# A 32-byte gap ahead of the pool that holds the two parts of the weights

## Chip, core and metric

The kernel runs on one core of one Trainium2 chip. The metric is device time in microseconds (us) of one execution, the median of several runs. TensorE (PE in the profile, PEld for its weight loads) multiplies, ScalarE (ACT) and VectorE (DVE) compute on what lies in SBUF and PSUM, and SyncE (SP) issues most transfers.

## What is computed

The reference is a trunk of two layers on one sequence of 256 tokens, model width 1024. All arrays are float32.

```
for l in range(2):
    x = x + 0.5 * swiglu(rmsnorm(x), w_gate, w_up, w_down)      # 1024 -> 2816 -> 1024
    h = rmsnorm(x)
    proj = h @ w_in          # [q | k | v | lru x | lru gate | memory q | 3 branch gates]
    A = window_attention(q, k, v)          # 8 heads of 64, 2 kv heads
    R = rg_lru(conv(lru x)) * gelu(lru gate)    # linear recurrence over tokens
    C = memory_attention(memory q, rmsnorm(mem) @ w_mem_kv)     # 4 heads of 128
    x = x + (g0 * (A @ w_attn_out) + g1 * (R @ w_lru_out) + g2 * (C @ w_mem_out)) @ w_out
    x = x + 0.5 * swiglu(rmsnorm(x), w_gate2, w_up2, w_down2)
return rmsnorm(x)
```

## The kernel before

Activations are kept feature-major: features on the 128 partitions, the 256 tokens along the row. Every large product is cut into weight blocks of 128 x 128. There are 3,456 of them, packed in the order of use in DRAM; eight stand side by side in a slab of 128 x 1024, so there are 432 slabs.

A product keeps float32 accuracy with two parts for each factor. A value is rounded to the type float32r (the "hi" part), and what is missing is a second float32r number (the "lo" part). A slab arrives in a stage tile `st` (line 179, from SP's queue, up to five slabs ahead). In `prep`, ScalarE writes `whi` (line 194) and VectorE then writes `wlo` (line 195), three slabs ahead of their use:

```
nc.scalar.activation(hi[:, c], st[:, c], AF.Copy)
nc.vector.tensor_tensor(lo[:, c], st[:, c], hi[:, c].bitcast(F32), op=ALU.subtract)
```

Activations are held by the class `Halves`: for each 128 features 256 columns of hi and beside them 256 of lo. `gemm` then spends two matmuls on a block (lines 219 and 220): hi weights against both parts of the activations (512 columns), and lo weights against the hi part (256 columns):

```
mm(both, hi, X.both(k), start=(k == 0), stop=False)
mm(out[:, 0, :], lo, X.hi(k), start=False, stop=(k == n - 1))
```

In both the weights are the stationary operand, which is loaded into the array (LDWEIGHTS in the profile, one ahead of each matmul), and the activations are the moving one, which streams through it a column at a time. Two more places use three matmuls of 256 columns on a block, again with the weights stationary: `singles` at the end (lines 236 to 238) and the gates of the recurrent branch (lines 675 to 677). In the memory's values (lines 622 to 624) it is the other way round: there the activations `xs` are stationary and 512 columns of weights move. The attention's own products (line 946 is one) are in plain float32, with neither operand in `whi` or `wlo`.

The order of the work is written out by hand: `block` prepares the slabs and advances a clock of tasks by one at each slab, and evictions, norms and attention hang on that clock.

Tiles lie in SBUF pool behind pool, in the order of the lines in `pools`, and every tile's row takes a multiple of 32 bytes. The first pool begins at byte 16,512 of a partition, which is a multiple of 64, and its first tile `pk` takes 1,056 bytes (16.5 times 64). From there on all large tiles begin 32 bytes past a multiple of 64: `whi` at 187,168 and four more at steps of 4,096, `wlo` at 207,648 and four more. The activations' tiles (21,792 and steps of 8,192) and the stage tiles (166,688 and steps of 4,096) do too. Blocks in a slab are 512 bytes apart, and parts of an activation tile 1,024 or 2,048, so no slice changes that remainder.

Of the kernel before, what the change touches and what calls it, by code (L numbers as in the profile page):

```python
# [19 lines left out]
F32 = mybir.dt.float32  # L20
# [74 lines left out]
class Trunk:  # L95
# [17 lines left out]
    def pools(self, ctx):  # L113
        tc = self.tc
        e = ctx.enter_context
        self.pc = e(tc.tile_pool(name="const", bufs=1))
        self.pbig = e(tc.tile_pool(name="big", bufs=14))
        self.ph4 = e(tc.tile_pool(name="h4", bufs=3))
        self.ps2 = e(tc.tile_pool(name="s2", bufs=4))
        self.ps1 = e(tc.tile_pool(name="s1", bufs=3))  # L120
        self.psm = e(tc.tile_pool(name="sm", bufs=2))
        self.pst = e(tc.tile_pool(name="stage", bufs=5))
        self.phl = e(tc.tile_pool(name="hl", bufs=5))
        self.pmm = e(tc.tile_pool(name="mm", bufs=3, space=bass.MemoryType.PSUM))
        self.patt = e(tc.tile_pool(name="att", bufs=2, space=bass.MemoryType.PSUM))
# [931 lines left out]
```

## Time and profile before

| | |
|---|---|
| runs | 1290.47, 1281.79, 1282.45 us; median 1282.45 |
| profiled execution, its own time | 1282.87 us |
| its span, first to last instruction | 1281.1 us |
| mean granted clock of TensorE | 0.997 of full |
| TensorE matmuls busy | 1265.4 us, 99% |
| weight loads (beside matmuls) | 1104.4 us, 86% |
| VectorE, ScalarE busy | 985.7 us (77%), 761.3 us (59%) |

The profiled execution lies 0.42 us (0.03%) above the median, and 1.8 us of it lie around its span. A matmul's record is longer than its share of the engine: records overlap, since the next matmul starts while the one before it drains. What a matmul costs is therefore read from the distance of two starts (its pitch), not from its record.

### The profile page before, as it was taken

Reading aid. Unit: us, or ns where it says so; the run is one execution under the profiler, and the core shown is the slowest. Engines: PE = TensorE matmul, PEld = TensorE weight load, DVE = VectorE, ACT = ScalarE, POOL = GpSimd, SP = SyncE. Lnnn points to the kernel's source line nnn. Section 1 sums busy time; section 2 is a strip of 40 time slices with the busy share of each in tenths; the row PEclk is TensorE's granted clock in tenths of the full one; section 3 lists DMA queues with packets and bytes.
Section 4 is the critical chain, followed back from the end, with each engine's and each line's share of the span. In section 5 each row is a group of like instructions: output and inputs, shape, how many; then the busy total and the mean of one; then the engine's idle time right before and its main releaser. Section 6 shows DMA issues by size and latency. Waiting matters only on the chain.

```text
span 1281.1 us, 19099 instructions
## 1 busy us (share of the span) xinstructions
PE 1265.4 (99%) x7318; PEld 1104.4 (86%) x7318; DVE 985.7 (77%) x1406; ACT 761.3 (59%) x1134; POOL 0.3 (0%) x5
## 2 busy tenths in 40 slices
PE   8999999999999999999999999999999999999997
PEld 7888888888888888888888888888888888888886
DVE  7788766888789987677678775669887898876754
ACT  5656544588577565555456564447867675655542
POOL 0000000000000000000000000000000000000000
PEclk9999999999999999999999999999999999999998
DMA  8665665555445566666656665564554465665651
GB/s 288 209 189 167 214 183 179 172 175 166 144 131 187 187 197 189 195 187 202 194 184 208 189 188 195 167 204 156 183 165 132 148 199 180 197 195 185 195 184 48
DMA packets 64748, 232.40 MB, mean 181 GB/s; under 512 B 7313, under 2 KB 7441, under 8 KB 64401
## 3 DMA queue, kind: packets, MB, share of 16 engines
q1 hardware_dynamic: 64224, 230.65, 57.2%
q8 instruction: 58, 0.95, 0.3%
q10 hardware_dynamic: 432, 0.53, 0.1%
q14 instruction: 34, 0.27, 0.1%
HBM read 230.10 MB, written 1.05 MB: 180 GB/s over the span
## 4 chain that ended last, share of the span: by engine, by line
PE 90%; DVE 5%; ACT 3%; issue 1%; DMA 1%; SPq 0%; DVEq 0%; ACTq 0%
PE pd L219 12%; PE pg L219 11%; PE pu L219 11%; PE pd L220 6%; PE pgt L219 6%; PE pu L220 6%; PE pg L220 6%; PE pbr L219 5%; PE pgt L220 3%; DVE wlo L195 2%; PE pyr L219 2%; PE pwo L219 2%; PE pbr L220 2%; PE pxr L219 2%; PE pgu L219 2%; PE pcq L219 1%
## 5 line engine op out<-in xcount | busy, mean ns | idle before, releaser
L195 DVE TENSOR_TENSOR wlo<-st,whi 128x1024 fp32r<-128x1024 f32 (+2 forms) x438 | 524.6, 1206 | 238.1 <-ACT whi L194 238.0
L194 ACT ACTIVATE whi<-st 128x1024 fp32r<-128x1024 f32 (+2 forms) x438 | 443.5, 1045 | 39.5 <-PE pd L219 20.5
L219 PE MATMUL pd<-h,whi 128*128 128x512 f32 x660 | 230.1, 393 | 0.0
L219 PE MATMUL pg<-xs,whi 128*128 128x512 f32 x640 | 225.2, 394 | 0.0
L219 PE MATMUL pu<-xs,whi 128*128 128x512 f32 x640 | 225.1, 393 | 0.0
L220 PE MATMUL pd<-h,wlo 128*128 128x256 f32 x660 | 184.9, 280 | 0.0
L220 PE MATMUL pg<-xs,wlo 128*128 128x256 f32 x640 | 179.3, 280 | 0.8 <-DVE wlo L195 0.8
L220 PE MATMUL pu<-xs,wlo 128*128 128x256 f32 x640 | 179.3, 280 | 0.0
L219 PEld LDWEIGHTS pd<-h,whi 128*128 128x128 f32 x660 | 123.6, 187 | 28.1
L219 PEld LDWEIGHTS pg<-xs,whi 128*128 128x128 f32 x640 | 119.9, 187 | 27.0
L219 PEld LDWEIGHTS pu<-xs,whi 128*128 128x128 f32 x640 | 119.8, 187 | 26.9
L219 PE MATMUL pgt<-xs,whi 128*128 128x512 f32 x384 | 139.2, 405 | 0.0
L220 PEld LDWEIGHTS pd<-h,wlo 128*128 128x128 f32 x660 | 124.7, 189 | 0.0
L220 PEld LDWEIGHTS pg<-xs,wlo 128*128 128x128 f32 x640 | 120.9, 189 | 1.1 <-DVE wlo L195 1.1
L220 PEld LDWEIGHTS pu<-xs,wlo 128*128 128x128 f32 x640 | 121.0, 189 | 0.0
L220 PE MATMUL pgt<-xs,wlo 128*128 128x256 f32 x384 | 107.6, 280 | 0.0
L219 PEld LDWEIGHTS pgt<-xs,whi 128*128 128x128 f32 x384 | 72.1, 188 | 19.5 <-issue 3.0
L258 ACT COPY g<-pg 128x512 f32<-128x512 f32 x40 | 23.5, 586 | 99.7 <-PE pg L220 92.9
L220 PEld LDWEIGHTS pgt<-xs,wlo 128*128 128x128 f32 x384 | 72.5, 189 | 0.2
L270 ACT ACTIVATE h<-u 128x512 fp32r<-128x512 f32 x44 | 27.8, 632 | 46.2 <-DVE u L523 43.9
L320 ACT ACTIVATE xs<-x,pk 128x256 fp32r<-128x256 f32 x40 | 18.7, 503 | 49.2 <-DVE x L559 21.6
L219 PE MATMUL pgu<-xs,whi 128*128 128x512 f32 x128 | 44.7, 394 | 1.2 <-DVE xs L324 1.2
(237 smaller groups left out, 2053.5 us busy)
## 6 DMA issues: line engine op xcount, KB each, us to landing
st<-wpack SPq DMA_DIRECT2D x428, 512.0 KB, 3.8
st<-wpack SPq DMA_DIRECT2D x8, 256.0 KB, 4.9
mem<-memT SPq DMA_DIRECT2D x2, 1024.0 KB, 6.7
x<-xT SPq DMA_DIRECT2D x4, 256.0 KB, 5.0
outT<-xg SPq DMA_DIRECT2D x2, 256.0 KB, 2.6
outT<-xg ACTq DMA_DIRECT2D x2, 256.0 KB, 2.7
cst<-cst SPq DMA_DIRECT2D x1, 320.0 KB, 7.8
pk<-pk SPq DMA_DIRECT2D x1, 128.0 KB, 7.5
```

Source lines behind the costliest of these rows:

```text
L194: nc.scalar.activation(hi[:, c], st[:, c], AF.Copy)
L195: nc.vector.tensor_tensor(lo[:, c], st[:, c], hi[:, c].bitcast(F32), op=ALU.subtract)
L219: mm(both, hi, X.both(k), start=(k == 0), stop=False)
L220: mm(out[:, 0, :], lo, X.hi(k), start=False, stop=(k == n - 1))
L258: self.nc.scalar.copy(dst, ps[:, :, 1, :])
L270: hi = lambda: self.nc.scalar.activation(X.hi(k, n), src, AF.Copy)
L320: self.t.nc.scalar.activation(self.xs.hi(k), x[:, k, :], AF.Copy, scale=self.t.vec(self.v, self.l, k))
```

## The change

One line is added to `pools`. It opens a pool of its own, with one tile of 8 float32 (32 bytes) in a partition that nothing reads or writes, between the stage tiles and the pool `hl` of the weights' parts.

```diff
         self.pst = e(tc.tile_pool(name="stage", bufs=5))
+        e(tc.tile_pool(name="gap", bufs=1)).tile([128, 8], F32, name="gap")
         self.phl = e(tc.tile_pool(name="hl", bufs=5))
```

In the built program `whi` then begins at 187,200 and `wlo` at 207,680 and at steps of 4,096 from there: multiples of 64. All tiles ahead of the pool keep their places, and nothing in SBUF lies behind it. The instructions, their order on every engine and what they wait for are the same as before; only the addresses in those that read or write `whi` and `wlo` differ.

## Rows read from the trace of the kernel before

**Rows 1.** The page: engines (busy, share of the span, instructions), and the chain by engine.
```profile
PE 1265.4 (99%) x7318; PEld 1104.4 (86%) x7318; DVE 985.7 (77%) x1406; ACT 761.3 (59%) x1134; POOL 0.3 (0%) x5
PE 90%; DVE 5%; ACT 3%; issue 1%; DMA 1%; SPq 0%; DVEq 0%; ACTq 0%
```

**Rows 2.** Busy time by windows, matmuls of line 219 alone, then line 220 alone, whole span.
```profile
0.00:1281.10 1281.10, 1164.72 (x3316) 621.52 (x3316) 1.00 0.58 181
0.00:1281.10 1281.10, 927.86 (x3316) 625.88 (x3316) 1.00 0.58 181
```

**Rows 3.** Timeline of TensorE at 576 us: start, length of the record, instruction.
```profile
575.71 0.39 PE L219 MATMUL pu<-xs,whi 128*128 128x512 f32 x1
575.94 0.28 PE L220 MATMUL pu<-xs,wlo 128*128 128x256 f32 x1
576.05 0.39 PE L219 MATMUL pu<-xs,whi 128*128 128x512 f32 x1
...
577.79 0.39 PE L219 MATMUL pu<-xs,whi 128*128 128x512 f32 x1
```

**Rows 4.** The same at 150 us.
```profile
149.76 0.40 PE L219 MATMUL pd<-h,whi 128*128 128x512 f32 x1
150.00 0.28 PE L220 MATMUL pd<-h,wlo 128*128 128x256 f32 x1
150.12 0.40 PE L219 MATMUL pd<-h,whi 128*128 128x512 f32 x1
...
150.82 0.40 PE L219 MATMUL pd<-h,whi 128*128 128x512 f32 x1
```

**Rows 5.** Windows, line 219: busy matmuls (count), loads (count), granted clock, DMA share, GB/s.
```profile
100.00:190.00 90.00, 90.00 (x255) 47.82 (x256) 1.00 0.60 188
500.00:640.00 140.00, 140.00 (x405) 75.55 (x404) 1.00 0.63 193
```

**Rows 6.** Timeline of TensorE, float32r matmuls of 512 columns alone (838 us).
```profile
837.84 0.39 PE L622 MATMUL mv<-whi,xs 128*128 128x512 f32 x1
838.07 0.39 PE L623 MATMUL mv<-wlo,xs 128*128 128x512 f32 x1
...
838.52 0.39 PE L622 MATMUL mv<-whi,xs 128*128 128x512 f32 x1
```

**Rows 7.** Timeline of TensorE, float32r matmuls of 256 columns alone (1262 us).
```profile
1262.12 0.28 PE L236 MATMUL pd<-h,whi 128*128 128x256 f32 x1
1262.24 0.28 PE L237 MATMUL pd<-h,whi 128*128 128x256 f32 x1
...
1262.48 0.28 PE L236 MATMUL pd<-h,whi 128*128 128x256 f32 x1
```

**Rows 8.** Plain float32: sixteen records in a timeline row, and the group of line 946.
```profile
367.55 3.62 PE L946 MATMUL mv<-MT,mkv 128*128 128x256 f32 x16
L946 PE MATMUL mv<-MT,mkv x32: 379/379/379, 367.6 to 998.7; 128*128 128x256 f32 x32
```

**Rows 9.** Groups of lines 236 and 675: count, duration ns least/median/most, first and last start.
```profile
L236 PE MATMUL pd<-h,whi x44: 279/283/283, 1254.2 to 1269.7; 128*128 128x256 f32 x44
L675 PE MATMUL lg<-xcs,whi x32: 279/283/285, 254.5 to 905.9; 128*128 128x256 f32 x32
```

**Rows 10.** The page's costliest groups: the two steps that write the weights' parts.
```profile
L195 DVE TENSOR_TENSOR wlo<-st,whi 128x1024 fp32r<-128x1024 f32 (+2 forms) x438 | 524.6, 1206 | 238.1 <-ACT whi L194 238.0
L194 ACT ACTIVATE whi<-st 128x1024 fp32r<-128x1024 f32 (+2 forms) x438 | 443.5, 1045 | 39.5 <-PE pd L219 20.5
```

**Rows 11.** TensorE's waits: who, for whom, us in total, times, longest.
```profile
PE rst L305 <- DVE r L298: 2.1, 2, 1.3
PE pg L220 <- DVE wlo L195: 0.8, 1, 0.8
PE pgu L220 <- DVE wlo L195: 0.2, 1, 0.2
```

## The prediction

> **What bounds the kernel now.** The page comes first: TensorE is busy for 1265.4 of 1281.1 us and the chain of waits lies on it for 90% [rows 1]. So at most 15.7 us of the span are idle time of TensorE. The list of its waits agrees: the longest entry is 2.1 us, and for the weights' parts it waits 1.0 us in all [rows 11]. No transfer and no other engine sets the end. What counts is how fast TensorE goes from one matmul to the next while it never waits, and that is read from the distance of the starts.
>
> Line 219 and line 220 have 3,316 matmuls each [rows 2], so 3,316 of the 3,456 blocks go through `gemm`. At 576 us six blocks take 577.79 - 575.71 = 2.08 us, 346.7 ns a block [rows 3]. At 150 us three blocks take 1.06 us, 353.3 ns a block [rows 4]. These are two steady paces, not noise. Between 500 and 640 us there are 404 starts of line 219 (405 records, one of them begun earlier), 140.00 / 404 = 346.5 ns. Between 100 and 190 us there are 254, 354.3 ns, at a granted clock of 1.00, its 2.4 GHz level, in both [rows 5]. The starts of line 219 through the whole trace, read in the same way, give 1,068 blocks at the longer pace, some 2,100 at the shorter, and about a hundred in between or at a stop. The rows above are samples of the two.
>
> What would a block cost if columns alone counted? Matmuls of 512 columns alone follow each other at 0.68 / 3 = 226.7 ns [rows 6], those of 256 columns at 0.36 / 3 = 120.0 ns [rows 7]. The difference is 106.7 ns for 256 columns, 0.417 ns a column, one at each beat of 2.4 GHz. That leaves 226.7 - 512 x 0.417 = 13.3 ns, and likewise 120.0 - 106.7 = 13.3 ns: **a surcharge of 13.3 ns for each matmul with its load**, whatever its length. A block of `gemm` has 768 columns, 320.0 ns, and two surcharges, 26.7: the 346.7 of the shorter pace. The longer pace has 6.7 ns more a block, which is the time of 16 columns, and 16 columns of float32 are 64 bytes of a row. The plain float32 matmuls, which have a load each too, show almost no surcharge: (3.62 - 0.379) / 15 = 216.1 ns [rows 8] for 256 columns at twice the column time, 213.3, so 2.7 ns. Their operands lie 32 bytes past a multiple of 64 as well. So neither a load as such nor that address costs 13 ns; the surcharge belongs to operands read at float32r's full rate.
>
> **The change part by part.** (1) The stationary operand of 3,316 x 2 matmuls in `gemm` [rows 2], 3 x 44 in the last product and 3 x 32 in the recurrent gates [rows 9] begins on a multiple of 64: 6,860 matmuls. In all but the 96 of lines 622 to 624 the moving operand keeps its place. Columns and loads stay as many. The open price is what the start of the stationary row does to the 13.3 ns, and the trace has no float32r load from a multiple of 64. Bounds from the nearest rows: at best the surcharge vanishes, 6,860 x 13.3 = 91.5 us; at worst it grows by the one quantum that the trace shows, 6.7 ns, for each load, 6,860 x 6.7 = 45.7 us more. I take zero. The reason is the evenness of the surcharge: it is exactly 32 columns' time where 128 weights are loaded for 256 columns and where they are loaded for 512, a whole fraction of the 128 weights. A load that paid for the 32 bytes by which its 512 bytes are out of step would rather show a remainder, 9 pieces of 64 bytes where 8 would do.
>
> The trace thus shows 13.3 ns for a load of 128 weights. The Trainium skill, on the page "TensorE: Matmul & The Clock Gate" in the section "Weight-path perf modes — Fast Weight Load (FWL) and DoubleRow", tells of a mode that fetches 128 weights as four parallel chunks of 32 columns, for types other than FP32. An estimate by that page is 32 columns, 13.3 ns, whatever the address, so zero from this change; the trace agrees in the number, though no row tells the type that the load is treated as. The page "SBUF — State Buffer", section "Door 1: The DMA port swizzle", has SBUF in lines of 16 bytes. By it 32 past a multiple of 64 is the start of a line already, and the same 32 lines are read before and after: zero again. What no row shows is whether TensorE reads in such lines.
>
> (2) Which of the two paces a stretch falls into may change. It is set after a stop and then kept: 254 blocks in 90 us without a return to the other [rows 5]. If every block went at the shorter pace, 1,068 x 6.7 = 7.1 us would be saved; I take zero and keep it for the range.
>
> (3) ScalarE writes `whi` and VectorE reads `whi` and writes `wlo` at the new addresses: 443.5 and 524.6 us in all [rows 10]. VectorE is idle for 1281.1 - 985.7 = 295 us and ScalarE for 520 [rows 1]. If both steps took a tenth more, 44 and 52 us, that would lie in this idle time; if a tenth less, TensorE's waits for them would lose a part of their 1.0 us [rows 11]. Nothing on the path, below half a microsecond on either side. The slabs have a margin: eight blocks at 346.7 ns take 2.8 us, a `wlo` 1.2.
>
> (4) The gap's tile is never used: zero instructions, no wait, no transfer.
>
> The sum against the profiled execution is 1282.9 + 0 = 1282.9 us; its distance to the median, 0.4 us, is kept, which gives 1282 us.
>
> **The rivals.** *A piece of 64 bytes less.* TensorE may fetch rows in pieces of 64 bytes. Out of step, a load needs nine pieces and the moving row one more as well, and the 13.3 ns would be two such extra pieces of 16 columns each. With the stationary row in step, one goes: 6.7 ns x 6,860 = 45.7 us, 1237 us. For it speaks that both paces are multiples of 16 columns' time above 768 (64 and 80) and that at half the rate, in plain float32, the surcharge is hidden. Against it speaks that the load's ninth piece need not stand in the way of the moving row at all. If only one of a block's two loads gains, it is half of that, 1260 us. If the whole surcharge hangs on the load's start, 91.5 us go, 1191 us; at that pace a slab takes 8 x 320 = 2.6 us, still above the 1.2 us of VectorE's step, so TensorE would remain the bound.
>
> *The longer pace everywhere.* Before, both streams begin 32 bytes past a multiple of 64, so their fetches keep one phase to each other. After it they are half a piece apart. If that makes load and stream collide once more a block, as in the stretches at 353.3 ns, then the 3,316 - 1,068 = 2,248 blocks that escape it now pay 6.7 ns: 15.0 us, 1297 us. It decides once more than about 85 in 100 of these blocks change (12.8 us are 1%). For it speaks that the longer pace exists and holds for long stretches; against it, that nothing in the rows ties it to an address: each stretch of rows 5 runs through over thirty slabs, through all five buffers of `whi`, at one pace. With one more collision at every load it would be 45.7 us, 1328 us.
>
> *The change doesn't do what it says.* Excluded: the addresses in the built program are multiples of 64.
>
> **How the numbers follow.** The surcharge stays, 1275 to 1290 us with some shift between the two paces: 46%. A piece less at each load, 1237 us: 21%; at one of two, 1260 us: 10%; all of it, 1191 us: 5%. The longer pace everywhere, 1297 us: 10%; a piece more at each load, 1328 us: 8%. The range from 1234 to 1299 us leaves out the two outer cases, 13%. A measurement of this kernel can tell about 1% (13 us) from no change: faster by more than that 36%, within it 46%, slower 18%.
>
> **What would show it.** In the changed kernel the starts of lines 219 and 220 decide alone. The forecast holds if matmuls of 256 columns in line 236 still follow at 120.0 ns and blocks at 346.7 or 353.3. The first rival shows as 113.3 ns in line 236 and 333.3 ns a block; the second as 353.3 everywhere at unchanged 120.0. Lines 622 to 624, where the weights move and `xs` is stationary, tell which stream pays: their 226.7 ns should stay if the stationary row's start matters alone. Lines 194 and 195 should keep 1,045 and 1,206 ns. What makes the forecast wrong is the reading of 32 columns as a price of the weights' count; it rests on one number that two mechanisms can give.

## The result, and the profile after

The changed kernel takes 1292.36 us (median of 6 runs, 1291.81 to 1295.65) against 1282.6 (6 runs, 1281.79 to 1290.47): 0.81% slower, ratio 1.0081, 95% interval 1.0064 to 1.0098. The forecast was 1282. The profiled execution took 1292.42 us, 9.55 more than that of before.

The page after, engines and the chain by engine, answers to [rows 1]:

```profile
PE 1275.7 (99%) x7318; PEld 1107.7 (86%) x7318; DVE 985.7 (76%) x1406; ACT 762.5 (59%) x1134; POOL 0.3 (0%) x5
...
PE 92%; DVE 4%; ACT 2%; issue 1%; DMA 1%; SPq 0%; DVEq 0%; ACTq 0%
```

TensorE has 10.3 us more of busy time, ScalarE 1.2 us more and VectorE the same as before. All line numbers behind the added line are one higher: `gemm` is now on lines 220 and 221. The groups of `prep` and TensorE's waits, after, answer to [rows 10, 11]:

```profile
L196 DVE TENSOR_TENSOR wlo<-st,whi 128x1024 fp32r<-128x1024 f32 (+2 forms) x438 | 524.7, 1206 | 247.6 <-ACT whi L195 247.0
L195 ACT ACTIVATE whi<-st 128x1024 fp32r<-128x1024 f32 (+2 forms) x438 | 444.6, 1047 | 40.4 <-PE pd L220 20.0
```
```profile
PE rst L306 <- DVE r L299: 2.0, 2, 1.3
...
PE pgu L221 <- DVE wlo L196: 0.2, 1, 0.2
```

Nothing there. The time is in the pitch of the blocks. The same two windows as [rows 5], matmuls of line 220:

```profile
100.00:190.00 90.00, 90.00 (x260) 48.68 (x261) 1.00 0.60 192
500.00:640.00 140.00, 140.00 (x397) 74.34 (x396) 1.00 0.60 190
```

The stretch at 100 us held 255 records and now holds 260, the one at 500 us held 405 and now holds 397. The two have changed places: one sped up, the other slowed down. The timeline of TensorE after shows the steps, at 576 us (against [rows 3]) and at 150 us (against [rows 4]):

```profile
575.85 0.40 PE L220 MATMUL pu<-xs,whi 128*128 128x512 f32 x1
...
576.21 0.39 PE L220 MATMUL pu<-xs,whi 128*128 128x512 f32 x1
...
576.55 0.40 PE L220 MATMUL pu<-xs,whi 128*128 128x512 f32 x1
...
577.26 0.40 PE L220 MATMUL pu<-xs,whi 128*128 128x512 f32 x1
```
```profile
149.88 0.39 PE L220 MATMUL pd<-h,whi 128*128 128x512 f32 x1
...
150.91 0.39 PE L220 MATMUL pd<-h,whi 128*128 128x512 f32 x1
```

Four blocks take 1.41 us at 576 us, in steps of about 0.36 and 0.35 in turn: 353 ns a block, where it had been 346.7. Three blocks take 1.03 us at 150 us, where they had taken 1.06; starts are shown to 10 ns, so the pace is better read from the window, 90.00 / 260 = 346 ns. Read through the whole trace by the prediction's count, the starts give (some twenty blocks next to restarts can be counted one way or the other):

| blocks | before | after |
|---|---|---|
| at 346.7 ns | 2,099 | 591 |
| at 353.3 ns | 1,068 | 2,557 |
| in between | 44 | 63 |
| at a stop | 52 (24.8 us) | 52 (24.0 us) |

Net, 1,489 more blocks at the longer pace are 1,489 x 6.67 = 9.9 us, the stops give back 0.8; the span grew by 9.5. By stretches (start in us: blocks at ns a block), those of 95 blocks and more:

```
before  30:103@353  76:375@353  221:96@353  397:207@347  476:511@347  660:511@347  849:96@353  1025:207@347  1103:435@347
after   29:103@353  76:375@347  218:96@347  394:207@353  474:511@353  661:511@353  854:96@353  1030:207@353  1110:435@353
```

Two stretches got better and five got worse. Within these stretches the pace never changes; they are separated by the plain float32 matmuls of norms and attention, or by a wait.

The matmuls of one length alone moved too. After, 512 columns (against [rows 6]) and 256 columns (against [rows 7]):

```profile
845.64 0.40 PE L623 MATMUL mv<-whi,xs 128*128 128x512 f32 x1
...
847.50 0.39 PE L625 MATMUL mv<-whi,xs 128*128 128x512 f32 x1
```
```profile
1270.05 0.28 PE L237 MATMUL pd<-h,whi 128*128 128x256 f32 x1
...
1270.76 0.28 PE L237 MATMUL pd<-h,whi 128*128 128x256 f32 x1
```

Eight matmuls of 512 columns in 1.86 us are 232.5 ns each (226.7 before), six of 256 in 0.71 us are 118.3 (120.0 before). With 213.3 and 106.7 ns for the columns, the surcharge that was 13.3 ns in both is now 19.2 in the one and 11.7 in the other. On the 96 and 132 matmuls concerned this makes 0.6 us more and 0.2 us less.

### The profile page after: what moved, and what is told of

Same layout as the page of the kernel before. It is cut to its first block, busy times and chain, and to the rows that moved or that the text cites. A ratio compares the mean times of both kernels' runs of the same rounds, so it can differ in the third digit from the quotient of the medians.

```text
span 1290.6 us, 19099 instructions
## 1 busy us (share of the span) xinstructions
PE 1275.7 (99%) x7318; PEld 1107.7 (86%) x7318; DVE 985.7 (76%) x1406; ACT 762.5 (59%) x1134; POOL 0.3 (0%) x5
## 4 chain that ended last, share of the span: by engine, by line
PE 92%; DVE 4%; ACT 2%; issue 1%; DMA 1%; SPq 0%; DVEq 0%; ACTq 0%
PE pd L220 12%; PE pg L220 11%; PE pu L220 11%; PE pgt L220 7%; PE pd L221 6%; PE pu L221 6%; PE pg L221 6%; PE pbr L220 5%; PE pgt L221 3%; PE pbr L221 2%; PE pyr L220 2%; PE pwo L220 2%; DVE wlo L196 2%; PE pgu L220 2%; PE pxr L220 2%; PE pwo L221 1%
## 5 line engine op out<-in xcount | busy, mean ns | idle before, releaser
L196 DVE TENSOR_TENSOR wlo<-st,whi 128x1024 fp32r<-128x1024 f32 (+2 forms) x438 | 524.7, 1206 | 247.6 <-ACT whi L195 247.0
L195 ACT ACTIVATE whi<-st 128x1024 fp32r<-128x1024 f32 (+2 forms) x438 | 444.6, 1047 | 40.4 <-PE pd L220 20.0
L220 PE MATMUL pu<-xs,whi 128*128 128x512 f32 x640 | 227.8, 397 | 0.0
```

## The experiments

**Theories.** Theory P said that two paces exist at any address, that a restart settles which one a stretch takes, and that a new address only deals the restarts anew. A restart here is the first block behind plain float32 matmuls or a wait. Its rival S said that the half piece of 64 bytes between stationary and moving rows brings on the longer pace. Later theories took up what was left of both. In every count below a block's pace is read as above.

**First round: other addresses, and one other restart.** Edits, each against the kernel before or after:

```diff
 e1_gap64 (after)
-        e(tc.tile_pool(name="gap", bufs=1)).tile([128, 8], F32, name="gap")
+        e(tc.tile_pool(name="gap", bufs=1)).tile([128, 16], F32, name="gap")
 e2_all64 (before)
+        e(tc.tile_pool(name="gap", bufs=1)).tile([128, 8], F32, name="gap")
         self.pbig = e(tc.tile_pool(name="big", bufs=14))
 e3_moving64 (after)
+        e(tc.tile_pool(name="gap0", bufs=1)).tile([128, 8], F32, name="gap0")
         self.pbig = e(tc.tile_pool(name="big", bufs=14))
 e4_before_extra (before), in rstd_b behind the loop
+        self.nc.tensor.matmul(ps[:, 256:264], r[:, 0:1].to_broadcast([128, 128]), self.ident[:, 0:8],
+                              start=True, stop=True)
```

> The gap is 64 bytes instead of 32, so the stationary rows lie 64 bytes further on than before the change and again 32 past a multiple of 64, like the moving rows. Theory P (pace): a stretch of blocks goes at 346.7 or 353.3 ns a block at any start address, which of the two is settled when it restarts after plain float32 matmuls, and a new address only deals these restarts anew; the time may then be anything between 1275 us (all at 346.7) and 1298 us (all at 353.3), and the long stretches at 353.3 are others than before. Theory S (step): it is the half piece between stationary and moving rows that brings on the longer pace; then this kernel is the one before, 1282 to 1283 us, with the stretches of 374 blocks at 76 us and 95 blocks at 221 us at 353.3 and those of 510, 510 and 434 at 346.7.

> The 32-byte gap stands ahead of the pool of the activations' large tiles, so moving and stationary rows both begin on multiples of 64. Theory P: 346.7 and 353.3 ns a block as ever, mixed anew, 1275 to 1298 us. Theory S: both rows in step with each other as before the change, 1282 to 1283 us with the stretches of before. The prediction's rival of pieces of 64 bytes: the moving row's extra piece goes, so a block takes 320 to 333 ns and the kernel 1190 to 1237 us.

> One 32-byte gap ahead of the activations' large tiles and a second one ahead of the weights' parts, so the moving rows begin on multiples of 64 and the stationary rows 32 past one. Theory P: 1275 to 1298 us, paces mixed anew. Theory S: half a piece apart as in the changed kernel, so about 1292 us, with 353.3 ns in the stretches of 510, 510 and 434 blocks. Rival of pieces: the moving row alone pays, 1237 us.

> The addresses of before; one more plain float32 matmul of 8 columns stands behind the two that broadcast each norm, its result read by nobody, so that the array restarts a few tens of ns later after each norm. It costs 9 places by less than 0.25 us, at most 2 us, if nothing else moves. Theory P: the stretches that begin behind a norm (374, 95, 510, 510, 434 blocks) are dealt anew, each change of pace worth 6.7 ns a block, 2.5 us for 374 and 3.4 us for 510 blocks; some of them now go at another pace than before. Theory S: addresses are unchanged, so all keep the pace of before and the time is 1282 to 1285 us.

| run | us | ratio to before (interval) | blocks at 346.7 / 353.3 |
|---|---|---|---|
| e1_gap64 | 1295.63 | 1.0102 (1.0072 to 1.0133) | 1 / 3,197 |
| e2_all64 | 1290.56 | 1.0061 (1.0031 to 1.0090) | 664 / 2,498 |
| e3_moving64 | 1294.45 | 1.0087 (1.0055 to 1.0119) | 245 / 2,885 |
| e4_before_extra | 1290.69 | 1.0048 (1.0021 to 1.0076) | 1,032 / 2,140 |

S falls twice: with 64 bytes the remainder is that of before, yet not one long stretch keeps the shorter pace; and e4, with no address changed, is 0.48% slower, and its 1,072 more blocks at the longer pace (7.1 us) account for the 7.2 us by which its span grew. The rival of pieces falls too: in e2, with all these rows on multiples of 64, no stretch goes below 346.7 ns a block. The windows of line 220, of e1_gap64 and then (line 219) of e4_before_extra:

```profile
500.00:640.00 140.00, 140.00 (x397) 74.48 (x397) 1.00 0.61 189
```
```profile
500.00:640.00 140.00, 140.00 (x398) 74.48 (x397) 1.00 0.61 188
1120.00:1200.00 80.00, 80.00 (x232) 43.20 (x231) 1.00 0.61 191
```

Eight small matmuls have turned the stretches of 511 blocks to the longer pace (397 records where [rows 5] had 405), and left the last one at the shorter (232 records in 80 us are 346 ns).

**Second round: counting restarts.** Nine long stretches are too few to tell odds from chance. A probe puts a plain float32 matmul of 4 to 97 columns ahead of every product of `pair`, 354 in all; its result is overwritten by the product.

```diff
+        self.restarts = 0
...
         for m in range(2):
+            n = 4 + 3 * (self.restarts % 32)
+            self.restarts += 1
+            self.nc.tensor.matmul(ps[:, m, 0, 0:n], self.ident, self.ident[:, 0:n], start=True, stop=True)
             self.gemm(ps[:, m, :, :], mk(m), X)
```

It runs on the addresses of before (p0), on those of the change (p32), of e1 (p64) and of e2 (q0); the last three, with all pools moved by 32 bytes (q1) and gaps of 96 and 128 bytes (p96, p128), came after the third round. Each probe was run once.

> A probe: ahead of each product of `pair` stands one more plain float32 matmul, of 4 to 97 columns in turn, into the part of the PSUM tile that the product overwrites. It adds some 350 restarts with different delays, so that the share of restarts which fall into each pace can be counted; the time itself is no matter (about 0.1 to 0.3 us for each restart, 1310 to 1390 us). Addresses of before: moving and stationary rows both 32 past a multiple of 64, a whole multiple of 128 apart. Theory P1: the share of restarts that fall into the longer pace (353.3 ns) is the same for every start address, some 60 to 75 in 100. Theory P2: the share depends on how far stationary and moving rows are apart (modulo 128), and is lowest here, a third to two thirds.

> The same probe with the gap of 32 bytes, so rows 32 bytes apart modulo 64. P1: the share of the longer pace as in the probe of before, within 8 in 100. P2: a clearly larger share, 80 to 90 in 100.

> The same probe with the gap of 64 bytes, so rows 64 bytes apart modulo 128. P1: the same share again. P2: nearly every restart at 353.3, over 95 in 100.

> The same probe with the gap ahead of the activations' tiles: both rows on multiples of 64, a multiple of 128 apart from each other as before. P1: the same share. P2, if it is the distance that counts: the share of the probe of before, within 8 in 100; if it is the remainder of the stationary row alone: that of the probe with the gap of 32 bytes.

> The probe of restarts with the 32-byte gap ahead of all pools: the constants (operands of the probe's own plain float32 matmul), the activations and the weights' parts all move by 32 bytes, so all distances are those of before and all rows now begin on multiples of 64. Theory D (distances between the rows count): the share of the longer pace is that of the probe of before, 52 in 100, with the longer pace at 34 columns and fewer and the shorter one above. Theory M (the remainder of each row by itself counts): as in the probe with both rows on multiples of 64, about 95 in 100.

> The probe with a gap of 128 bytes ahead of the weights' parts. If rows count modulo 128: the share of before, 52 in 100, with the same table by columns. If modulo 256 or more: some other share.

> The probe with a gap of 96 bytes: stationary rows on multiples of 64 as in the changed kernel, but in the other half of 128 bytes. If the remainder modulo 64 counts: as with the gap of 32, 68 in 100 at the longer pace, a quarter in between and 6 at the shorter. If modulo 128: some other table.

Measured, for stretches of seven and more blocks, as counts at the shorter pace / in between / at the longer one (shorter: mean below 348.3 ns, longer: above 351.5; right behind a restart a mean of six blocks is a little off):

```
columns of the restart     4-34      37     40-58    61-64     67-97   all stretches     us
p0   before               1/0/95   7/0/2   44/0/15   1/0/14   93/0/6    153/0/169    1360.93
q1   every row +32        1/0/95   7/0/2   44/0/15   1/0/14   93/0/6    153/0/168    1362.39
q0   not the constants    2/1/93   7/0/2    0/0/59   1/0/14    0/0/99    16/1/304    1366.10
p32  weights +32          0/1/95   9/0/0   0/31/28   0/9/6     0/39/60   19/83/219   1366.01
p64  weights +64          0/0/96   0/0/9    0/0/59   0/0/15    0/0/99     0/1/320    1365.68
p96  weights +96          95/1/0   8/1/0    54/5/0   15/0/0    89/10/0   301/20/0    1353.60
p128 weights +128         0/96/0   0/9/0    0/59/0   0/15/0    0/99/0     0/321/0    1361.71
```

Four things follow. The restart's length decides: at the addresses of before, 4 to 34 columns lead to the longer pace in 95 of 96 cases and 67 to 97 to the shorter in 93 of 99. The address decides as well, against P1: 52 in 100 at the longer pace before, 99.7 with 64 bytes, none with 96. Third, q1 repeats p0 for all 278 restarts that stand right behind the added matmul, one by one: moving all pools by 32 bytes changes nothing, so remainders modulo 64 do not count and distances do (theory D; M falls, and so does S once more). The constants' rows belong to these distances, since q0 leaves them behind and loses the shorter pace, but for one case, above 37 columns. Fourth, 32 and 96 differ, and so do 0 and 128, so distances don't repeat after 64 or 128 bytes. At 128 every stretch is in between, at about 350 ns a block. P2 was thus right that the share depends on the distance and wrong in "modulo 128": its lowest share is at 96 bytes and not at 0, p32 has 68 in 100 at the longer pace and not 80 to 90, and q0, with 95, has neither of the two shares that P2 named for it.

**Third round: the pace set on purpose.** If restart and distance settle the pace, it should be possible to turn a stretch by the length of one small matmul. `pair` gets an argument that puts one ahead of a product, at eight places (the third gate product of each feed-forward part, the second `pxr`, the second output pair):

```diff
-    def pair(self, nm, mk, X):
+    def pair(self, nm, mk, X, restart=False):
         ps = self.mm(nm)
+        if restart:
+            self.nc.tensor.matmul(ps[:, 0, 0, 0:91], self.ident, self.ident[:, 0:91], start=True, stop=True)
...
-                g = gate(self.pair("pg", kb("w_gate", fp), norm.xs))
+                g = gate(self.pair("pg", kb("w_gate", fp), norm.xs, fp == 2))
...
-            conv(p, self.pair("pxr", w(C_XR, p), norm.xs))
+            conv(p, self.pair("pxr", w(C_XR, p), norm.xs, p == 1))
...
-                self.join(t, self.pair("pbr", mk, X), gated)
+                self.join(t, self.pair("pbr", mk, X, p == 1 and nm == "w_attn_out"), gated)
```

with 91 or 16 columns at the addresses of before, 37 with the change, 91 with the gap of 64.

> Addresses of before. Eight restarts are set on purpose: one plain float32 matmul of 91 columns ahead of the third gate product of each feed-forward part, of the second product of the recurrent branch and of the second output pair of the merge. In the probe with these addresses all 10 restarts of that length led to 346.7 ns a block. Theory R (the pace is settled by the delay of the last restart together with the addresses): the stretches behind the eight go at 346.7 ns; of the 1,068 blocks at the longer pace in the profile before, the 374 and about 160 more leave it, 3.6 us less, against 8 x 0.22 = 1.8 us of added work: 1281 us, and little scatter. Theory A (the addresses alone set the odds): the time is that of before plus 1.8 us, 1284 to 1286 us, with both paces behind the eight.

> The same eight restarts, with 16 columns instead of 91; in the probe with these addresses all 8 restarts of that length led to 353.3 ns. Addresses and instructions are those of the kernel with 91, but for the length of eight matmuls. Theory R: all long stretches behind the eight go at 353.3 ns, some 2,900 blocks in all, 12.4 us above the profile before, 1296 us, 15 us slower than with 91 columns although less is computed. Theory A: as with 91 columns or a fraction of a microsecond faster.

> The changed kernel (gap of 32 bytes) with the same eight restarts at 37 columns. In the probe with the gap, 37 columns were the one length that led to 346.7 ns in all 9 cases. Theory R: the long stretches behind the eight return to 346.7 ns, of the 2,557 blocks at the longer pace some 1,900 leave it, 12.4 us less than the changed kernel, 1.6 us of work more: 1281 to 1282 us, the time of the kernel before. Theory A: 1293 to 1295 us.

> The gap of 64 bytes with the eight restarts at 91 columns. In the probe with that gap 320 of 321 restarts led to 353.3 ns. Theory R with that table: everything stays at 353.3 ns, 1297 us, that is the 1295.6 us of that gap without restarts plus 1.7 us. If a long restart freed the pace at any address: 1281 us as with the addresses of before.

| run | us | ratio to before (interval) | blocks at 346.7 / 353.3 | of the eight places at 346.7 |
|---|---|---|---|---|
| f0_restart91 | 1285.69 | 1.0033 (1.0021 to 1.0046) | 1,954 / 1,189 | 5 |
| f0_restart16 | 1293.59 | 1.0095 (1.0080 to 1.0111) | 619 / 2,519 | 0 |
| f32_restart37 | 1284.45 | 1.0028 (1.0015 to 1.0041) | 1,749 / 1,358 | 5 |
| f64_restart91 | 1297.09 | 1.0123 (1.0108 to 1.0139) | 1 / 3,182 | 0 |

The windows of line 219, from 500 to 640 us and from 1125 to 1200 us, of f0_restart91, then of f0_restart16, then (line 220) of f32_restart37:

```profile
500.00:640.00 140.00, 140.00 (x405) 75.55 (x404) 1.00 0.60 193
1125.00:1200.00 75.00, 75.00 (x218) 40.44 (x217) 1.00 0.63 193
```
```profile
500.00:640.00 140.00, 140.00 (x397) 74.41 (x396) 1.00 0.60 189
1125.00:1200.00 75.00, 75.00 (x214) 39.93 (x213) 1.00 0.59 184
```
```profile
500.00:640.00 140.00, 140.00 (x405) 75.85 (x404) 1.00 0.61 193
1125.00:1200.00 75.00, 75.00 (x217) 40.61 (x217) 1.00 0.61 191
```

With the addresses of before, 16 columns cost 7.9 us more than 91. And the changed kernel, with 37 columns at eight places, is 7.9 us faster than without them (1292.36, in another round; against the kernel before of its own round it is 0.28% slower instead of 0.81%), although it does more: what the gap costs lies mainly in its paces. Theory A falls. The size was off, in f0_restart16 too (1293.59, not 1296): the four places in feed-forward parts went as the probe said in all four runs, those in the merge and the branch only once with 91 columns (of four) and once with 37. So f0_restart91 is at 1285.69 and not 1281: with its eight matmuls added it has 1,189 blocks at the longer pace, no fewer than the 1,068 of before. Why those places did not follow is open. In p0 all 7 stretches of `pxr` behind 67 and more columns went at the shorter pace, yet behind 91 columns here both of its stretches stayed at the longer one; column count and distance are thus not all that counts. The stretch of 375 blocks has no added restart right ahead of it, and yet it changed too: it went at 353 ns in f0_restart91 (as before the change) and f32_restart37 (347 after the change), and at 347 ns in f0_restart16 (353 before).

**Fourth round: a distance that leaves no choice.** The edit, against the changed kernel:

```diff
-        e(tc.tile_pool(name="gap", bufs=1)).tile([128, 8], F32, name="gap")
+        e(tc.tile_pool(name="gap", bufs=1)).tile([128, 24], F32, name="gap")
```

and with 40 and 56 float32 for 160 and 224 bytes.

> The change with a gap of 96 bytes instead of 32, without any added restart. Theory D (the distance between stationary and moving rows decides, together with the restart): in the probe with this gap no restart of 321 fell into the longer pace, so every stretch goes at 346.7 ns; the 1,068 blocks at 353.3 of the profile before save 7.1 us: 1275 to 1277 us, faster than the kernels before and after the change, with little scatter. If the remainder of the stationary rows modulo 64 decided: as the changed kernel, 1292 us.

> A gap of 160 bytes, so 128 further than the changed kernel. If distances count modulo 128: as the changed kernel, about 1292 us with most long stretches at 353.3 ns. If modulo 256 or more, as the probe with 128 suggests: some other mixture of paces, between 1275 and 1298 us.

> A gap of 224 bytes, 128 further than the gap of 96. If distances count modulo 128: as that kernel, 1275 to 1277 us, all stretches at 346.7 ns. If modulo 256 or more: some other mixture, between 1275 and 1298 us.

g96 takes 1276.65 us (1276.30 to 1276.78, 5 runs) beside 1282.87 for the kernel before: ratio 0.9953 (0.9941 to 0.9966), faster than the kernels before and after the change by 6.2 and 15.7 us (the second across rounds). 3,172 blocks go at 346.7 ns and 7 are counted at the longer pace, though no stretch of more than three blocks has a mean above 348.3. g224 does the same, 1276.51 us, 0.9953 (0.9939 to 0.9966), 3,139 blocks and none. g160 takes 1287.44, 1.0039 (1.0024 to 1.0055), and shows a third pace, 350.0 ns, in every stretch of 95 blocks and more. The windows of g96 and the timeline of g160, line 220:

```profile
100.00:190.00 90.00, 90.00 (x261) 48.68 (x261) 1.00 0.60 192
...
500.00:640.00 140.00, 140.00 (x405) 75.83 (x404) 1.00 0.61 192
```
```profile
575.63 0.39 PE L220 MATMUL pu<-xs,whi 128*128 128x512 f32 x1
...
575.98 0.39 PE L220 MATMUL pu<-xs,whi 128*128 128x512 f32 x1
...
577.73 0.39 PE L220 MATMUL pu<-xs,whi 128*128 128x512 f32 x1
```

g96 holds 261 and 405 records in the two windows; of before and after the better numbers were 260 and 405. In g160 six blocks take 2.10 us, 350.0 ns each. So 96 does come back at 224, while 32 (two paces, mostly the longer) does not at 160 (one pace of its own). A distance of 256 bytes was not run.

**The streams that have one pace only.** The matmuls of one length alone show what the distance does without any choice of pace. Their mean pitch through the whole trace, by the distance of the weights' parts from the activations (bytes added to that of before), in all twenty executions:

| bytes added | 0 | 32 | 64 | 96 | 128 | 160 | 224 |
|---|---|---|---|---|---|---|---|
| executions | 8 | 4 | 3 | 2 | 1 | 1 | 1 |
| 256 columns, ns | 119.9-120.0 | 118.3-118.4 | 117.8 | 117.3 | 118.7 | 120.0 | 116.7 |
| 512 columns, ns | 227.6-227.9 | 233.1-233.2 | 229.4 | 233.2-233.3 | 232.4 | 234.0 | 233.1 |

e2, q0 and q1 stand with the kernel before, and e3 with the changed kernel, although remainders modulo 64 and the constants' places differ. Sixty matmuls of 256 columns in e2_all64 (7.20 us, 120.0 ns each), then in e3_moving64 (7.09 us, 118.2), all behind the last write to `wlo`:

```profile
1269.84 0.28 PE L237 MATMUL pd<-h,whi 128*128 128x256 f32 x1
...
1277.04 0.28 PE L237 MATMUL pd<-h,whi 128*128 128x256 f32 x1
```
```profile
1273.59 0.28 PE L238 MATMUL pd<-h,whi 128*128 128x256 f32 x1
...
1280.68 0.28 PE L238 MATMUL pd<-h,whi 128*128 128x256 f32 x1
```

This speaks against a rival that no run was made for: with the gap the weights' parts also move away from the stage tiles, and writes by ScalarE, VectorE or transfers might meet TensorE's reads otherwise. Here nothing more is written to the weights' parts, and the two pitches are those of the whole product. For the long stretches that rival is not tested by itself.

## Why the prediction was wrong

**What bounds the kernel** was right: TensorE paces everything, 1275.7 of 1290.6 us after, and the time moved with its pitch but for 0.8 us of stops.

**The step that failed is part (2)**, "Which of the two paces a stretch falls into may change ... I take zero and keep it for the range". It named what happened and mis-sized it. It gave it one side only, the 7.1 us to be gained; the other side, 2,248 blocks that could get worse, stood with the rival of the longer pace. What came is two thirds of that rival: 1,489 x 6.67 = 9.9 us out of 15.0. The sum should have carried -7.1 to +15.0 us for this term. The argument that "nothing in the rows ties it to an address" rested on five buffers of `whi` that lie 4,096 bytes apart. They could not show what 32 bytes do; it only seemed to be evidence. The runs showed in its place that the pace hangs on the distance of the rows together with the restart: with 64 bytes all long stretches go at 353.3 ns, with 96 all at 346.7.

**The rival's mechanism** (rows half a piece apart collide once more) is not what the runs show. With 64 bytes the rows are whole pieces apart and every block is at the longer pace; with 96 they are half a piece apart and none is.

**Part (1), the surcharge,** was right for a block at its shorter pace, 346.7 ns at every gap of 0, 32, 96 and 224 bytes. The reason given, 32 columns' time as a price of the number of weights, fell: matmuls of one length now pay 11.7 and 19.2 ns. The prediction called this reading its weakest point, and by its own signs, 120.0 ns in line 236 and 226.7 in lines 622 to 624, it failed there; but that is worth 0.4 us of the 9.5. An estimate by the Trainium skill's page "TensorE: Matmul & The Clock Gate", section "Weight-path perf modes — Fast Weight Load (FWL) and DoubleRow", was 32 columns' time, 13.3 ns, at any address; the trace does not agree beyond the addresses of before. The Trainium skill's page "SBUF — State Buffer", section "Door 1: The DMA port swizzle", has SBUF in lines of 16 bytes. If only such lines counted, moving a row by four whole lines, 64 bytes, would change nothing; e1_gap64 is 1.02% slower. Neither covers what depends on the distance of two rows. **The rival of pieces of 64 bytes** has no support: no stretch at 333.3 ns a block was seen at any address. **Parts (3) and (4)** held: 1,047 and 1,206 ns for `prep` (1,045 and 1,206 before), no new wait.

**What stays open** is the mechanism below: which accesses meet when the stationary, moving and constants' rows have a certain distance, and how a restart can lock a stretch of 500 blocks into it. The runs tell that distances and restarts move the pace, not by what, and the places in the third round that did not follow show that something else counts as well. The kernel before, 46 runs in all, scattered from 1278.93 to 1293.56 us, g96 from 1276.30 to 1276.78 in 5; that restarts fall otherwise from run to run at a distance that allows two paces would give this, but of the kernel before only one execution was profiled, so it is argued and not shown. Right behind the probe's own matmuls the pace did not vary: p0 and q1, two executions, agree in 278 of 278 cases.

## What to carry to other kernels

When a kernel is bound by TensorE, read the distance of starts stretch by stretch; two steady paces in one trace are a sign that the price of a matmul hangs on something that the next edit may move, as it did here. A sum that takes such a pace over from before has to carry both ways for all the blocks concerned. Where float32r weights and activations stream for hundreds of microseconds, try the distance between their pools in steps of 32 bytes: here it is worth 1.5% from the best (96 and 224) to the worst (64), and at 96 and 224 the long stretches have no other pace left to fall into.

## What the runs showed of the hardware

- Float32r matmuls with their loads have several steady paces for the same work: 346.7, 350.0 and 353.3 ns for a block of 768 columns, which is 64, 72 and 80 columns' time above the columns, at a granted clock of 1.00 in all.
- A pace once taken lasted through 510 blocks, across tiles, products and eviction. Before and after the change no stretch of 95 blocks and more changed its pace in the middle; in e3_moving64 a stretch of 71 blocks at 370 us did, from 353 to 347 ns.
- At the addresses of before, a plain float32 matmul that is 3 columns longer turned the pace of what follows: behind 34 columns 9 of 9 stretches took the longer pace, behind 37 columns 7 of 9 the shorter; behind 61 and 64 columns 14 of 15 the longer again.
- The table of restarts came back for 278 of 278 cases when all rows were moved by the same 32 bytes.
- Float32r matmuls of one length have a mean pitch that follows the distance of their two rows: 116.7 to 120.0 ns for 256 columns and 227.6 to 234.0 for 512, the same to 0.3 ns in all executions at one distance.
